# Reordering the first pass of a two-layer encoder kernel: c as one row, casts and loads in another order, eight gate dots moved into attention 0

## The chip, the cores and the metric

The kernel runs on one core of a Trainium2 chip. The metric is device time in microseconds (us), the median of three executions. The engines of a core work side by side and meet through semaphores: TensorE (PE; its weight loads are PEld), VectorE (DVE), ScalarE (ACT), GpSimd (POOL) and SyncE (SP), whose queue issues nearly all DMA transfers of this kernel.

## The reference

A trunk of two layers works on x (1024 tokens of 1024 values) with a conditioning vector c (1024 values). For layer i:

```
mod = silu(c) @ ada_w[i] + ada_b[i]          # 3 x 1024 values
shift, scale, gate = split(mod, 3)
h = rmsnorm(x, norm_g[i]) * (1 + scale) + shift
y = branch_i(h)                               # 0: differential attention, 1: latent attention
x = x + gate * y
```

Branch 0 projects h to q, k, v and z (1024 values each), rotates q and k by a position-dependent angle, takes for each of 8 heads the difference of two softmaxes, norms the result of each head, multiplies by silu(z) and projects out. A last RMSNorm closes the trunk. All data are float32.

## The kernel before, in words

A float32 product is made of three matmuls of a high and a low part in the `fp32r` format: high x high, high x low, low x high. So every operand is first split: ACT casts the high part, and POOL or VectorE subtracts it to get the low part (for weights L229/L230 and L547/L548, for h L493 to L498).

**The order of work.** The program text is the request; a scheduler then fixes the order of the instructions on each engine when the kernel is built, and `tc.issue_after(x)` asks it to place an instruction behind instruction x. At run time each engine takes its instructions in that fixed order and stops at the first one whose inputs are not ready. The SP queue works the same way: a DMA waits there for a free buffer and holds up what stands behind it. Tiles with a `tag` and `bufs=n` share n buffers in turn.

**First pass (L549 to L645).** It makes h for the first 512 tokens and, chunk by chunk of 128 channels (loop variable k), multiplies it into V for those tokens (`vacc`, four PSUM banks) and into the first half of the first K strip (`kacc`).

- c is loaded as 128 copies of one row (L424), tanh and one VectorE step make silu(c) times 2 (L427, L428), and ACT copies it into PSUM (`cb`, L559).
- x comes as four tiles of 128 tokens x 1024 (`load_x`). The sum of squares of each is taken on ACT or VectorE (`sq_x`), one POOL instruction makes the four inverse roots (`inv_rms`, `rsqrt`, L171), ACT scales the first 256 channels of each tile (L567), VectorE the other 768 (L621).
- For each k two weight tiles `ada` (512 KB each, four buffers) come in, and two dot products with c on VectorE (`mod_dot`, L434, inside `mod_pair`) give the shift and the scale of that chunk's 128 channels.
- `h_chunk` transposes the four tiles' channels of chunk k on PE (L488, bank `trh`) and makes h from them on ACT, twice: `h0h`, the high part (L493), and `h`, full precision (L495); POOL subtracts (`h0l`, L498). The V weights of chunk k are cast and subtracted as `wvh`, `wvl`.
- PE then does eight matmuls with h0h (L638, L639), two for K (L640, L641), four with h0l (L643) and one more for K (L644). The matmuls lag one chunk behind the transposes (SKEW).
- After the last chunk's dots VectorE turns positions into angles (`angles`, L575 to L592) and ACT takes three sines; the tables go to HBM and come back spread over partitions.

**After it.** The Q weights (`wq0`) are split and the Q strip of the first half is multiplied (`strip_half`, L184 to L186, into `acc`), for which the first `vacc` bank must be empty: `store_v` casts it on ACT (L361), subtracts on VectorE (L362) and stores it. The second 512 tokens are two tiles `xt` and two tiles cut in halves `xth`; their squares are all taken on ACT, all four inverse roots made at once and all of them scaled on VectorE (`norm_x`, L477). Then follow chunk by chunk their h and V.

**V stage.** The other half of V (weights `wv1`, outputs `vps`) is made tile by tile (`v0_tile`), beside K and Q strips of head 0. `gen_mods` runs along: one `mod_dot` of VectorE and one 512 KB load at each step, first 16 for layer 1's shift and scale, then 8 for layer 0's gate (`gen_gate`); MODS says how many steps go ahead of each V tile.

**Attention 0 (`attn0`, `q_tile`).** For each tile of 128 queries of a head PE makes two score tiles (L773, banks `sc`, two of them), VectorE takes the maximum of each (L399), ACT the exponential (L401), and VectorE combines the two (reciprocal L779, L780, combine L781). The result is transposed on PE (L382), moved out on ACT (`pth`, L384) and VectorE (`ptl`, L385), and multiplied with V (`pv`) for two tiles together. Between these, PE gets matmuls of the next head's strips as filling. `extra`, if given, is called after each tile. `mk["V"]` holds the last marked VectorE instruction, and `behind("V")` asks for a place behind it. Later stages (output projections, layer 1, attention 1) are not touched.

Of the kernel before, what the change touches and what calls it, by code (L numbers as in the profile page):

```python
# [21 lines left out]
P = 128  # L22
# [23 lines left out]
MODS = (2, 2, 2, 2, 3, 2, 0, 0)  # L46
# [14 lines left out]
VB = (2, 3)  # L61
WV1 = 6
ADA_B = 4
X1_AT = 6
WQ_AT = 6
# [3 lines left out]
X_CUT = 256  # L69
FIN_LAG = 1  # L70
# [15 lines left out]
def trunk(ctx: ExitStack, tc: tile.TileContext, A, out):  # L86
# [96 lines left out]
    def mm3(psum, ah, al, bh, bl, first, last):  # L183
        PE.matmul(psum, ah, bh, start=first, stop=False)  # L184
        PE.matmul(psum, ah, bl, start=False, stop=False)  # L185
        PE.matmul(psum, al, bh, start=False, stop=last)  # L186
# [17 lines left out]
    def fetch_strip(srcs, nks):  # L204
        raws = []
        for src, nk in zip(srcs, nks):
            raw = wst.tile([P, HF], F32, name="wraw", tag="wraw", bufs=2)
            SP.dma_start(raw[:, : nk * P], src)
            raws.append((raw, nk))
        return raws  # L210
# [148 lines left out]
    def store_v(l, sp, acc, tt, fh, tag="vst", bufs=None):  # L359
        v = sp.tile([P, 2, HF], F32R, name="v_hl", tag=tag, bufs=bufs or VB[l])  # L360
        S.copy(v[:, 0, :], acc)  # L361
# [54 lines left out]
    def mod_load(src, mp, nb, tag="ada"):  # L416
        w = mp.tile([P, D], F32, name="ada", tag=tag, bufs=nb)
        SP.dma_start(w, src)
        return w

    def load_c(pl, th, **kw):

        c2 = pl.tile([P, D], F32, name="c2", **kw)
        SP.dma_start(c2, A["c"].to_broadcast([P, D]))  # L424

        def fin():
            S.activation(th, c2, AF.Tanh, scale=0.5)  # L427
            V.scalar_tensor_tensor(out=c2, in0=th, scalar=1.0, in1=c2, op0=ALU.add, op1=ALU.mult)  # L428

        return c2, fin  # L430
# [13 lines left out]
    def gen_gate(l, load, c2):  # L444

        gcol = sm.tile([P, KT], F32, name="gcol", tag="gcol", bufs=1)
        for j in range(KT):
            mod_dot(load(A[f"ada_g{l}"][j]), part(f"ada_bg{l}")[:, j : j + 1], gcol[:, j : j + 1], c2)
            if j == KT - 1:
                SP.dma_start(gateS[l].rearrange("(p j) -> p j", p=P), gcol)  # L450
            yield

    def gen_mods(load, c2):
# [8 lines left out]
        yield from gen_gate(0, load, c2)  # L462
# [16 lines left out]
    def h_chunk(l, xn4, k, dst, hp, sub=G, wide=False, act=False, f32=None):  # L479
# [13 lines left out]
        S.activation(hh, tr[:, :n, :], AF.Identity, bias=bk, scale=ak)  # L493
        if act:
            S.activation(tmp, tr[:, :n, :], AF.Identity, bias=bk, scale=ak)  # L495
# [15 lines left out]
    st1 = ExitStack()  # L511
    p1 = pool(st1, "p1a")

    def load_x(half):

        xs = []
        for j in range(4):
            if half == 1 and j > 1:
                xs.append([wp.tile([P, HF], F32, name="xth", tag="rp", bufs=6) for _ in range(2)])
            else:  # L520
                xs.append([p1.tile([P, D], F32, name="xt", tag="xt", bufs=6)])
            for i, x_ in enumerate(xs[j]):
                n = D // len(xs[j])
                SP.dma_start(x_, A["x"][half * 4 + j, :, i * n : i * n + n])
        return xs

    def sq_x(xs, on_act=range(4)):
        ss = sm.tile([P, 4], F32, name="xss")
        for j, x_ in enumerate(xs):
            for i, piece in enumerate(x_):  # L530
                dst = ss[:, j : j + 1] if i == 0 else sm.tile([P, 1], F32, name="xs2")
                if j in on_act:
                    junk = p1.tile([P, D], BF16, name="junk", tag="junk", bufs=1)
                    S.activation(junk[:, : piece.shape[1]], piece, AF.Square, accum_out=dst)
                else:
                    junk = p1.tile([P, D], BF16, name="junk2", tag="h32", bufs=2)
                    V.tensor_tensor_reduce(out=junk, in0=piece, in1=piece, scale=1.0, scalar=0.0, op0=ALU.mult, op1=ALU.add, accum_out=dst)
                if i:
                    V.tensor_add(ss[:, j : j + 1], ss[:, j : j + 1], dst)
        return ss  # L540

    def load_wv(l, k, fh, src, eng=G):
        raw = p1b.tile([P, HF], F32, name="wvr", tag="wvr", bufs=2)
        SP.dma_start(raw, src)
        h_ = p1b.tile([P, HF], F32R, name="wvh", tag="wv", bufs=16)
# [5 lines left out]
    psum("ps1", accx=3, tr=1, cb=1)  # L551
    th = p1.tile([P, D], F32, name="cth", tag="ada", bufs=ADA_B)
    c2, c_fin = load_c(p1b, th)
    xs0 = load_x(0)
    posi = p1.tile([P, 256], I32, name="posi", tag="rot", bufs=3)
    SP.dma_start(posi, A["pos"])
    c_fin()
    cb = bank("cb", "cb", [P, D])
    S.copy(cb, c2)  # L559

    def ada0(j):
        return [mod_load(A["ada_ss0"][j, i], p1, ADA_B) for i in range(2)]

    wm0 = ada0(0)
    y0 = inv_rms(sq_x(xs0, X_ACT0), 4)
    for j in range(4):
        S.mul(xs0[j][0][:, :X_CUT], xs0[j][0][:, :X_CUT], y0[:, j : j + 1])  # L567


    tabS = [dr.tile([4, 32, 256], F32, name=f"tabS{i}") for i in range(3)]  # L570

    def angles():
        ang = p1.tile([P, 256], F32, name="ang", tag="rot", bufs=3)
        kk = p1.tile([P, 256], F32, name="kk", tag="rot", bufs=3)
        V.tensor_copy(ang, posi)  # L575
        V.tensor_scalar(ang, ang, inv[:, 0:1], None, op0=ALU.mult)
        MAGIC = float(1.5 * 2 ** 23)
# [6 lines left out]
        for C in (C1, C2, C3):  # L584
            V.scalar_tensor_tensor(out=ang, in0=kk, scalar=-C, in1=ang, op0=ALU.mult, op1=ALU.add)
# [24 lines left out]
    for k in range(-1, KT + SKEW):  # L610
# [11 lines left out]
        if k == KT - 1:  # L622
            with tc.issue_after(m_last):
                angles()
# [1218 lines left out]
```

## Time and profile before

| | us |
|---|---|
| median of three runs | 1441.18 |
| lowest and highest | 1438.9, 1443.01 |
| the profiled execution | 1438.65 |
| its span | 1436.9 |

The span runs from the first to the last instruction of the profiled execution. A row of a timeline holds start, length, engine, line, operation, output<-input, shapes and, in brackets, how long the engine had stood idle and what ended that. A row of the waits holds who waited for whom, the total in us, how often, and the longest.

### The profile page before, as it was taken

What the parts mean: (1) busy time and instruction counts of PE and PEld (TensorE: products, weight loads), DVE (VectorE), ACT (ScalarE), POOL (GpSimd) and SP (SyncE); (2) the same over time, 40 slices, a digit from 0 to 9 for tenths busy, and PEclk for the clock granted to TensorE, in tenths of its full rate; (3) what the DMA queues carried; (4) which work ended last, traced back from release to release, by engine and by line L of the source; (5) the groups of instructions that cost most, each with busy time, mean ns of one, the idle gap of its engine ahead of it and who ended that gap; (6) DMA issues with size and microseconds to landing.
All of it is one profiled execution on the core that took longest, in us unless ns stands there. A gap on an engine that the chain in (4) does not pass through costs nothing. (4 is left out here: it accounts for less than half of the span.)

```text
span 1436.9 us, 20644 instructions
## 1 busy us (share of the span) xinstructions
PE 1388.8 (97%) x7388; PEld 1158.8 (81%) x7388; DVE 917.5 (64%) x1372; ACT 728.7 (51%) x1287; POOL 610.6 (42%) x483
## 2 busy tenths in 40 slices
PE   5999999999999999998999999999999999999997
PEld 4778788888888888887787877887888888888886
DVE  6656877767777767677435985545666555555355
ACT  5622375666565656566343452335455554545342
POOL 4416164656464646464461343532141331412572
PEclk9999999999999999999999999999999999999999
DMA  8787723333332333237653145398343432336563
GB/s 326 238 254 237 255 70 93 84 104 81 96 101 84 96 89 91 86 96 248 236 183 125 38 132 184 122 305 236 133 130 111 130 101 77 104 96 217 185 237 136
DMA packets 135527, 213.70 MB, mean 149 GB/s; under 512 B 19072, under 2 KB 56064, under 8 KB 135424
## 3 DMA queue, kind: packets, MB, share of 16 engines
q1 hardware_dynamic: 135424, 212.38, 47.1%
q8 instruction: 58, 0.95, 0.3%
q14 instruction: 45, 0.37, 0.1%
HBM read 137.92 MB, written 50.80 MB: 131 GB/s over the span
## 5 line engine op out<-in xcount | busy, mean ns | idle before, releaser
L384 ACT CAST pth<-tr 128x512 fp32r<-128x512 f32 x256 | 150.6, 588 | 284.2 <-PE tr L382 281.9
L399 DVE TENSOR_REDUCE nm<-s 128x1 f32<-128x1024 f32 x192 | 234.1, 1219 | 77.2 <-PE s L773 65.7
L385 DVE TENSOR_TENSOR ptl<-tr,pth 128x512 fp32r<-128x512 f32 x256 | 176.2, 688 | 139.4 <-ACT pth L384 138.9
L230 POOL TENSOR_TENSOR wl<-wraw,wh 128x512 fp32r<-128x512 f32 (+2 forms) x79 | 103.6, 1314 | 205.6 <-ACT wh L229 183.4
L401 ACT ACTIVATE e<-s,nm 128x1024 f32<-128x1024 f32 x128 | 143.7, 1123 | 29.8 <-DVE nm L399 29.2
L382 PE MATMUL tr<-ident,e 128*128 128x128 f32 x1024 | 155.1, 274 | 2.3 <-DVE ptl L385 2.0
L382 PEld LDWEIGHTS tr<-ident,e 128*128 128x128 f32 x1024 | 121.2, 140 | 43.6 <-DVE ptl L385 19.2
L184 PE MATMUL acc<-h0h,wh 128*128 128x512 f32 x360 | 150.1, 417 | 1.9 <-DVE v_hl L362 1.8
L184 PE MATMUL pv<-pth,vt 128*128 128x256 f32 x512 | 147.1, 287 | 0.0
L185 PE MATMUL pv<-ptl,vt 128*128 128x256 f32 x512 | 145.8, 285 | 0.0
L186 PE MATMUL pv<-pth,vt 128*128 128x256 f32 x512 | 144.7, 283 | 0.0
L186 PE MATMUL acc<-h0h,wl 128*128 128x512 f32 x360 | 143.1, 398 | 0.5 <-POOL wl L230 0.5
L185 PE MATMUL acc<-h0l,wh 128*128 128x512 f32 x360 | 142.0, 394 | 0.0
L1013 POOL TENSOR_TENSOR wol<-wor,woh 128x512 fp32r<-128x512 f32 x64 | 85.0, 1351 | 84.7 <-ACT woh L1012 77.2
L185 PEld LDWEIGHTS pv<-ptl,vt 128*128 128x128 f32 x512 | 97.6, 191 | 2.9
L184 PEld LDWEIGHTS pv<-pth,vt 128*128 128x128 f32 x512 | 97.4, 190 | 2.9 <-ACT pth L384 0.2
L186 PEld LDWEIGHTS pv<-pth,vt 128*128 128x128 f32 x512 | 97.6, 191 | 0.1
L326 POOL TENSOR_TENSOR rp_r<-rp_raw,cosT 128x512 f32<-128x512 f32 x38 | 49.8, 1311 | 91.0 <-ACT rp_raw L321 50.8
L331 POOL TENSOR_TENSOR rp_sw<-rp_sw,sinT 128x512 f32<-128x512 f32 x42 | 55.4, 1318 | 74.1 <-DMA rp_sw<-rp_raw 73.9
L773 PE MATMUL s<-ks,qa 128*128 128x512 f32 x256 | 82.6, 404 | 2.8 <-DVE e L781 2.6
L781 DVE SCALAR_TENSOR_TENSOR e<-s,z,e 128x1024 f32<-128x1024 f32 x64 | 82.1, 1283 | 2.1
L773 PE MATMUL s<-ks,qb 128*128 128x512 f32 x256 | 81.1, 395 | 0.0
(590 smaller groups left out, 3335.4 us busy)
## 6 DMA issues: line engine op xcount, KB each, us to landing
ada<-in_ada_ss SPq DMA_DIRECT2D x32, 512.0 KB, 6.0
wraw<-in_w_s SPq DMA_DIRECT2D x64, 256.0 KB, 2.9
vS<-v_hl SPq DMA_DIRECT2D x32, 512.0 KB, 5.9
vt<-vS SPq DMA_DIRECT2D x32, 512.0 KB, 3.7
wor<-in_w_out SPq DMA_DIRECT2D x64, 256.0 KB, 3.9
rp_sw<-rp_raw SPq DMA_DIRECT2D x168, 64.0 KB, 2.0
bc_s<-bc_d SPq DMA_DIRECT2D x34, 256.0 KB, 4.1
oS<-bc_s SPq DMA_DIRECT2D x30, 256.0 KB, 2.5
```

The costliest lines, as they stand in the source:

```text
L184: PE.matmul(psum, ah, bh, start=first, stop=False)
L185: PE.matmul(psum, ah, bl, start=False, stop=False)
L186: PE.matmul(psum, al, bh, start=False, stop=last)
L230: sub = (V if pair_of else G).tensor_sub(l_[:, :n], raw[:, :n], f32v(h_[:, :n]))
L382: PE.transpose(tr[:, j, :], p[:, kt * P : (kt + 1) * P], ident)
L384: mk["S"] = S.copy(pth[kh][:, :, dst], tr).ins
L385: mk["V"] = V.tensor_sub(ptl[kh][:, :, dst], tr, f32v(pth[kh][:, :, dst])).ins
L399: mk["V"] = V.reduce_max(nm, s_ps, axis=AX.X, negate=True).ins
L401: mk["S"] = S.activation(e, s_ps, AF.Exp, bias=nm, scale=1.0, accum_out=zs).ins
L773: PE.matmul(s_ps[:, kc * HF : (kc + 1) * HF], src[:, c, ql], KS[h][kc][:, c, :], start=fst, stop=not fst)
L781: combined.append(V.scalar_tensor_tensor(out=e0, in0=e1, scalar=z1[:, 0:1], in1=e0, op0=ALU.mult, op1=ALU.add).ins)
L1013: in_turn(G.tensor_sub(lo, raw, f32v(hi)))
```

## The change

- **c.** It is loaded as one row of 4 KB (`crow`), silu is made on that row, and two matmuls with a row of ones spread it over 128 partitions into `cb`. A copy `c2` back to SBUF is made later, on ACT in chunk 5. Eight matmuls of ones are put ahead of the spread and nine behind it (`keep_busy`, WARM); their results are not used.
- **x, first half.** Squares and inverse roots are made for three tiles together, and for the fourth alone, with its square in two halves, one on ACT and one on VectorE. Of VectorE's four scalings two are placed behind the first pair of dots and two behind the second.
- **Angles and sines.** The positions are loaded in chunk 0; the VectorE steps are dealt out over five chunks, the sines over chunks 4, 5 and 7 (SIN_AT).
- **Order of loads and casts.** Many loads and casts get an `issue_after`: V and K weights are split behind the h of the chunk before, the Q weights are loaded ahead of the second half's x, and the V weights wv1 from the fourth on are split behind the copies of the V banks.
- **x, second half.** The squares of the first two tiles go to VectorE, those of the other two stay on ACT; inverse roots and scalings are made for each pair by itself, and the second half of the channels of the second pair is scaled on ACT.
- **Gate dots.** The eight dots of layer 0's gate leave the V stage and are called from attention 0, one after every fifth tile, through `extra`. c2 and two load buffers get a pool of their own (`pg`) that stays open until attention 0 is over.
- VB gives V's stores three buffers instead of two, and the scratch for dynamic DMAs is set to 1024.

```
-MODS = (2, 2, 2, 2, 3, 2, 0, 0)
+MODS = (2, 1, 1, 1, 0, 0, 0, 0)
-VB = (2, 3)
-WV1 = 6
+VB = (3, 3)
+WV1 = 3
+WARM = (8, 9)
+SIN_AT = (4, 5, 7)
...
+    def sq_halves(pieces, dst):
+        other = sm.tile([P, 1], F32, name="xs2")
+        sq_piece(pieces[0], dst, True)
+        sq_piece(pieces[1], other, False)
+        V.tensor_add(dst, dst, other)
...
-    c2, c_fin = load_c(p1b, th)
-    xs0 = load_x(0)
+    warm = bank("acc", "warm")
+    SP.dma_start(crow[0:1, :], A["c"])
+    xs0 = [load_x(0, 0)]
+    xs0 += [load_x(0, j) for j in range(1, 4)]
+    keep_busy(WARM[0])
...
+    c_act = S.activation(th[0:1, :], crow[0:1, :], AF.Tanh, scale=0.5).ins
+    c_last = V.scalar_tensor_tensor(out=crow[0:1, :], in0=th[0:1, :], scalar=1.0, in1=crow[0:1, :], op0=ALU.add, op1=ALU.mult).ins
+    cb = bank("cb", "cb", [P, D])
+    for f in range(2):
+        fs = slice(f * HF, f * HF + HF)
+        spread = PE.matmul(cb[:, fs], ones[0:1, :], crow[0:1, fs], start=True, stop=True).ins
+    with tc.issue_after(spread):
+        keep_busy(WARM[1])
...
+    y_ = inv_rms(ss0[:, 0:3], 3)
+    for j in range(3):
+        y0[j] = y_[:, j : j + 1]
+        S.mul(xs0[j][0][:, :X_CUT], xs0[j][0][:, :X_CUT], y0[j])
+    sq_halves([xs0[3][0][:, :HF], xs0[3][0][:, HF:]], ss0[:, 3:4])
+    y0[3] = inv_rms(ss0[:, 3:4], 1)[:, 0:1]
...
             with tc.issue_after(m_last):
-                for j in range(4):
-                    V.tensor_scalar(xs0[j][0][:, X_CUT:], xs0[j][0][:, X_CUT:], y0[:, j : j + 1], None, op0=ALU.mult)
-        if k == KT - 1:
+                x_rest(0)
+                x_rest(1)
+        if k == 0:
             with tc.issue_after(m_last):
-                angles()
+                x_rest(2)
+                x_rest(3)
...
+            if k >= 0:
+                with tc.issue_after(m_last):
+                    next(angle_steps, None)
...
+            if k + 1 < KT:
+                with tc.issue_after(h_chunk.act):
+                    wv0.append(split_wv(vraw))
+            if k in SIN_AT:
+                sines(SIN_AT.index(k))
...
-    norm_x(sq_x(xs1), xs1)
+    norm_x(ssa, xs1[:2])
+    yb = inv_rms(ssb, 2)
+    for j in range(2):
+        V.tensor_scalar(xs1[2 + j][0], xs1[2 + j][0], yb[:, j : j + 1], None, op0=ALU.mult)
+        S.mul(xs1[2 + j][1], xs1[2 + j][1], yb[:, j : j + 1])
...
+    def gate_steps0():
+        gcol = sm.tile([P, KT], F32, name="gcol", tag="gcol", bufs=1)
+        yield
+        w = []
+        for j in range(KT):
+            while len(w) < min(2, KT - j):
+                with tc.issue_after(mod_load.last):
+                    w.append(mod_load(A["ada_g0"][j + len(w)], pg, 2))
+            for _ in range(5):
+                yield
+            js = slice(j, j + 1)
+            with behind("V"):
+                mod_dot(w.pop(0), part("ada_bg0")[:, js], gcol[:, js], c2)
+        SP.dma_start(gateS[0].rearrange("(p j) -> p j", p=P), gcol)
+
+    gate0 = gate_steps0()
     for h in range(NH - 1):
-        attn0(h, lambda i: FILL0[i])
+        attn0(h, lambda i: FILL0[i], lambda i: next(gate0, None))
```

201 lines of the change are left out of this document (117 added, 84 removed).

## The prediction

> **What bounds the kernel now.** I read the page's busy shares first, then busy time by stage, then what TensorE waited for, then the timeline around each wait. Columns of the stage table: stretch, length, busy time of PE, PEld, DVE, ACT, POOL, granted clock, DMA share, GB/s.
>
> ```profile
> PE 1388.8 (97%) x7388; PEld 1158.8 (81%) x7388; DVE 917.5 (64%) x1372; ACT 728.7 (51%) x1287; POOL 610.6 (42%) x483
> ...
> 14.46:23.30 8.84, 7.75 (x24) 5.04 (x24) 8.77 (x13) 5.19 (x10) 5.96 (x4) 1.00 0.86 324
> 49.17:55.06 5.89, 3.69 (x10) 2.38 (x10) 2.56 (x6) 4.73 (x13) 1.26 (x1) 0.71 0.61 184
> 300.00:350.00 50.00, 50.00 (x280) 42.55 (x279) 33.53 (x50) 30.72 (x54) 30.76 (x26) 1.00 0.31 89
> ...
> PE trh L488 <- ACT xt L567: 14.5, 1, 14.5
> PE vacc L643 <- POOL h0l L498: 2.1, 1, 2.1
> ...
> PE vps L184 <- ACT wvh L547: 0.7, 1, 0.7
> ...
> PE vps L185 <- DVE wvl L548: 0.2, 1, 0.2
> ```
>
> PE is busy 97% of the span, so only its idle time and its slow matmuls can be won. The change touches the front: 14.5 us before the first transpose, a stretch to 23.3 us with VectorE full (8.77 of 8.84) and PE half empty, and a hole at 49 us. In attention 0 PE has no idle time, while VectorE is busy for two thirds: whatever is moved there has to fit into VectorE's gaps.
>
> **The change part by part. The start.**
>
> ```profile
> 3.00:6.00 3.00, 0.00 (x0) 0.00 (x0) 0.00 (x0) 0.00 (x0) 0.00 (x0) 1.00 0.97 231
> 6.00:9.00 3.00, 0.00 (x0) 0.00 (x0) 1.45 (x2) 2.58 (x4) 0.00 (x0) 1.00 1.01 410
> 11.23 1.23 DVE L537 CUSTOM_DVE_ANT_0 junk<-xt 128x1024 bf16<-128x1024 f32 x1 [1.22 <-DMA xt<-in_x]
> 12.82 1.04 POOL L171 TENSOR_TENSOR rq_y<-xss,mhalf 128x4 f32<-128x4 f32 x1 [11.54 <-DVE xss L466]
> 13.90 1.71 ACT L567 ACTIVATE xt<-xt,rq_y 128x256 f32<-128x256 f32 x4 [2.67 <-POOL rq_y L171]
> 15.52 0.62 DVE L621 TENSOR_SCALAR xt<-xt,rq_y 128x768 f32<-128x768 f32 x1
> 16.20 1.59 POOL L548 TENSOR_TENSOR wvl<-wvr,wvh 128x512 fp32r<-128x512 f32 x1 [2.34 <-ACT wvh L547]
> 18.14 1.64 DVE L621 TENSOR_SCALAR xt<-xt,rq_y 128x768 f32<-128x768 f32 x1
> 22.28 1.27 DVE L434 CUSTOM_DVE_ANT_0 ada<-ada,cb,vec 128x1024 f32<-128x1024 f32 x1
> 22.46 0.78 ACT L493 ACTIVATE h0h<-trh,modb,moda 128x512 fp32r<-128x512 f32 x1 [3.29 <-DVE moda L442]
> 23.30 0.50 PE L638 MATMUL vacc<-wvh,h0h 128*128 128x512 f32 x1 [0.18 <-ACT h0h L493]
> 27.28 0.39 PE L638 MATMUL vacc<-wvh,h0h 128*128 128x512 f32 x1
> 43.89 1.39 DVE L575 CAST ang<-posi 128x256 f32<-128x256 int32 x1
> 52.44 0.64 ACT L534 ACTIVATE junk<-xth 128x512 bf16<-128x512 f32 x1
> 52.98 0.19 ACT L534 ACTIVATION_READ_ACCUMULATOR junk<-xth 128x1 f32 x1
> ```
>
> The spread copy of c (512 KB) goes; 4 KB take its place. At 410 GB/s its bytes are 1.3 us; but the engines were full at 231 GB/s from 3 to 6 us, another 1.3 us lost to slow packets. I take 2.3 us (bounds 1.3 and 2.6): the last token tile, awaited until 11.23, lands at 8.9. Its square is now cut in halves of 512 columns (0.64 and 0.19 on ACT, the other half beside it on VectorE); the inverse root for three tiles and then that for the fourth each take POOL 1.04, so the fourth tile is scaled at 12.5 (four scalings took 1.71, one 0.43) against 15.6. The first pair of dots (2 x 1.27 and small steps) starts when its first weights land, 512 KB or 1.3 us behind x at 10.2, and ends at 13.25.
>
> From there VectorE's order decides. Two scalings of the rest of x (0.62, and 1.64 next to a POOL instruction, as in the rows): 15.5. The second pair, 2.75: 18.3, against 22.4 before (ACT got the result at 22.46). But then come, ahead of the third pair, the cast of the positions (1.39), two more scalings (0.62 and 1.64) and one small step (0.35): 4.0, so 22.3; third pair 25.1; the h of the third chunk 0.8 later. The transposes of the third chunk stand in PE's order behind three matmuls of the second and need all four scalings, so PE, which reaches them at about 20.2, idles for 2.1 us. The third chunk's matmuls start at 26.0 against 27.28: gain **1.3 us**, not the 3 that the second chunk would have had. Bounds: with c worth only 1.3 us, 0.3; with no contention between POOL and VectorE, some 3. The 17 warm matmuls, the two that spread c, the rows of c on ACT and VectorE and the copy of c out of PSUM lie in time in which those engines have nothing else, and cost nothing; the SP queue has one DMA as before. The wait of the vS store, and of loads ordered behind others, holds nothing that PE needs within its 2 us lead.
>
> **The end of the first half.** From the third to the eighth chunk PE has no gap before (27.28 to 46.74, five chunks, 3.89 each) and I leave that: the eighth starts at 45.5.
>
> ```profile
> 46.74 0.39 PE L638 MATMUL vacc<-wvh,h0h 128*128 128x512 f32 x1
> 48.78 0.39 PE L641 MATMUL kacc<-h0h,wl 128*128 128x512 f32 x1
> 49.12 0.76 ACT L495 ACTIVATE h<-trh,modb,moda 128x512 f32<-128x512 f32 x1
> 51.28 1.93 PE L643 MATMUL vacc<-wvh,h0l 128*128 128x512 f32 x4 [2.10 <-POOL h0l L498]
> 51.96 0.59 ACT L361 CAST v_hl<-vacc 128x512 fp32r<-128x512 f32 x1 [1.16 <-PE vacc L643]
> 52.00:53.00 1.00, 1.00 (x3) 0.71 (x3) 0.42 (x1) 1.00 (x3) 0.00 (x0) 0.50 0.75 178
> 52.58 0.69 DVE L362 TENSOR_TENSOR v_hl<-vacc,v_hl 128x512 fp32r<-128x512 f32 x1 [2.89 <-ACT v_hl L361]
> 53.73 0.79 PE L184 MATMUL acc<-h0h,wq 128*128 128x512 f32 x1
> 59.96 0.38 PE L488 MATMUL trh<-ident,xt 128*128 128x128 f32 x2
> 61.43 0.50 PE L184 MATMUL vacc<-wvh,h0h 128*128 128x512 f32 x1 [0.43 <-ACT h0h L493]
> ```
>
> Before, ACT made the last h at 49.12, behind squares and sines, POOL followed, PE stood 2.1 us and then ran at a granted clock of 0.50. The change puts sines and casts of the weights into earlier chunks and the squares behind the h. What is late next is the emptying of the first V bank (ACT 0.59, DVE 0.69), which the Q matmuls wait for. From the start of the eighth chunk: ten matmuls of 0.23, the first of the last four 0.39, then 0.59 and 0.69 with 0.1 between: 4.2 us to the first Q matmul, against 6.99 (46.74 to 53.73): gain **2.75**. The 24 Q matmuls at full clock take 24 x 0.233 = 5.6 us against 6.23: **0.6**.
>
> **The pairs of the second half.**
>
> ```profile
> 56.40 1.01 POOL L171 TENSOR_TENSOR rq_y<-xss,mhalf 128x4 f32<-128x4 f32 x1 [5.17 <-DVE xss L466]
> 58.78 1.67 DVE L477 TENSOR_SCALAR xth<-xth,rq_y 128x512 f32<-128x512 f32 x4
> ```
>
> The second pair's four squares (0.64 and 0.19 each, as above) stand on ACT between the bank copies (0.58), so they can't start before the V banks are done: 8.3 us after the eighth chunk's start; sums, POOL's 1.01 and two scalings of 0.42 bring it to 10.8, while PE is through with Q at 9.8. Then two more scalings and a bank copy stand on ACT before the first h (12.55). From the last Q matmul to the first V matmul: 2.75 us against 1.47 (59.96 to 61.43): **-1.3**. The first pass together: 1.3 + 2.75 + 0.6 - 1.3 = 3.35 us.
>
> **The V stage.** Eight dots (10.9 us of VectorE) and 4 MB leave it. Two of its waits hang on V weights that were fetched late (0.7 and 0.2, the two vps rows above); the Q half now stands ahead of them on PE. A third (1.13) is for the emptying of a bank, which stood on VectorE behind gate dots and a reduction:
>
> ```profile
> 159.65 0.50 PE L184 MATMUL acc<-h0h,wh 128*128 128x512 f32 x1 [1.13 <-DVE v_hl L362]
> ```
>
> Gain **2.0** if all three go (bounds: 0, where other waits follow in their place, and these 2.0).
>
> **The dots in attention 0.** Eight of 1.36 us (with the read), one in every fifth tile, placed between the second evacuation of a tile and the reciprocal that waits for ACT's exponential.
>
> ```profile
> 190.46 0.16 DVE L779 RECIPROCAL z<-z 128x1 f32<-128x1 f32 x1 [0.41 <-ACT s L401]
> 310.09 1.28 DVE L781 SCALAR_TENSOR_TENSOR e<-s,z,e 128x1024 f32<-128x1024 f32 x1
> 311.99 0.63 PE L773 MATMUL s<-ks,qa 128*128 128x512 f32 x2
> ```
>
> In the usual tile VectorE waits 0.41 us there, so the combine (L781) is moved by 1.0. Half of the dots fall on a tile after which PE has its P x V matmuls (24) and needs that bank only 4 us later: free. Behind the other four the next scores follow the combine's end by about 0.6 (310.09 + 1.28 to 311.99): 0.4 to 0.5 us each, unless the tile already had spare time. I take **-1.0** (bounds: 0, and 8 x 1.36 = -10.9). The loads (8 of 512 KB at a DMA share of 0.31) are hidden; each waits on SP for a buffer that the dot of two turns earlier freed.
>
> **Sum.** 3.35 + 2.0 - 1.0 = 4.35 us. The profiled execution took 1438.65 (span 1436.9); 1434.3. It lies 2.5 below the median of the runs, 1441.18; so 1436.8 for the median.
>
> **The clock, by page and by row.** The hole of 2.1 us at 49 us was followed by 0.50; a hole as long at 891 us was not:
>
> ```profile
> 893.01 0.50 PE L186 MATMUL zacc<-t2h,wl 128*128 128x512 f32 x1 [2.12 <-POOL wl L230]
> ```
>
> [...]
>
> **Rivals.**
> 1. *The clock drops in the new holes.* A drop lasts about 3.6 us at half speed, as from 51.3 to 55.0: 1.85 us lost. One or both of them take the first pass to 1.5 or -0.4; with V and dots the gain is 0.6 to 2.5: 1439.6. For it: the 2.1 us hole is as long as the one that had it. Against: the hole at 891.
> 2. *The dots stall attention 0.* Place: VectorE between evacuation and reciprocal; price: up to 1.36 each, since the next reduction, the exponential and the evacuation of the one transpose bank all queue behind it. Slower than before from 0.67 us a dot on (5.35 / 8); at the full price 10.9 - 5.35 = 5.5 slower: 1446.7. For it: PE has no slack of its own there. Against: half of the places have 4 us.
> 3. *The start is better than worked out.* If POOL and VectorE do not collide behind the second pair and the token chain keeps its 2.3 us, the third chunk starts at 24.2, 1.8 earlier, and the pairs' squares run ahead (1.3 back): 1433.7.
> 4. *The change does nothing where it aims:* the last h still comes late, behind the casts of the Q weights that stand ahead of it on ACT (1.13), if those land late: the 2.75 goes, 1439.6.
>
> **Chances.** Forecast 0.50 (its own range 1434 to 1439), rival 1 0.15, rival 2 0.11, rival 3 0.16, rival 4 0.08. 0.3% (4.3 us) is about what a measurement of this kernel can tell from no change. Faster by more: half of the forecast, rival 3 and a little of the others: 0.45; slower by more: rival 2, and a little: 0.12; within: 0.43. The range goes from 1430.5 (rival 3 with all V waits gone and no stall) to 1443 (rival 1 with 0.6 us a dot), leaving 0.2 out.
>
> **What the profile after would show.** The first chunk's h near 13.5 us; a PE wait for x's scalings near 20 to 22; the third chunk from 26; no POOL wait before the last four V matmuls, the first Q matmul near 50 with clock 1.00; a wait of 1 us for xth at 56; no wait for V weights near 90; short waits of the scores for the combine in attention 0, at every other dot. Wrong would make me: a clock under 1.00 at 22 or 58, a late landing of the last modulation weights, or more than 3 us of PE idle in attention 0.

## The result, and the profile after

The changed kernel took 1437.68 us (median of 14 runs, 1434.67 to 1441.94) against 1441.66 for the kernel before (14 runs, 1438.72 to 1445.61): 4.0 us less, a ratio of 0.9970 (95% interval 0.9958 to 0.9982). The forecast was 1436.8, 4.4 less than before. Its profiled execution took 1437.65 (span 1435.9), right at its median, while the profiled execution of before (1438.65) was shorter than any of those 14; the two profiles differ by 1.0 us only, and the medians tell the truer difference.

The page's busy shares of the changed kernel:

```profile
PE 1398.5 (97%) x7426; PEld 1165.9 (81%) x7426; DVE 921.5 (64%) x1377; ACT 727.2 (51%) x1287; POOL 612.9 (43%) x485
```

Its busy time by stage, the same stretches and columns as in the prediction:

```profile
14.46:23.30 8.84, 7.92 (x36) 5.85 (x37) 8.77 (x16) 3.68 (x8) 6.66 (x6) 1.00 1.03 393
49.17:55.06 5.89, 5.89 (x29) 4.79 (x28) 3.50 (x10) 4.60 (x11) 0.70 (x1) 1.00 0.79 206
300.00:350.00 50.00, 50.00 (x283) 42.71 (x283) 36.71 (x56) 30.42 (x54) 30.86 (x26) 1.00 0.31 85
```

Between 14.46 and 23.30 TensorE now issues 36 matmuls where it issued 24; at 49 us the hole and the half clock are gone (5.89 of 5.89 busy, clock 1.00); from 300 to 350 us, in attention 0, VectorE has 3 us more work and TensorE still no idle time.

The timeline of the start of the changed kernel, then that of the end of the first half (start, length, engine, line and operation; in brackets the idle time before and what ended it):

```profile
9.10 0.69 DVE L513 CUSTOM_DVE_ANT_0 junk<-xt 128x512 bf16<-128x512 f32 x1 [1.28 <-DMA xt<-in_x]
13.69 0.78 ACT L473 ACTIVATE h0h<-trh,modb,moda 128x512 fp32r<-128x512 f32 x1 [0.59 <-DVE xt L605]
18.93 0.28 DVE L561 CAST ang<-posi 128x256 f32<-128x256 int32 x1
19.13 0.61 DVE L605 TENSOR_SCALAR xt<-xt,rq_y 128x768 f32<-128x768 f32 x1
19.66 0.34 DVE L562 TENSOR_SCALAR ang<-ang,vec 128x256 f32<-128x256 f32 x1
19.92 0.61 DVE L605 TENSOR_SCALAR xt<-xt,rq_y 128x768 f32<-128x768 f32 x1
24.11 0.50 PE L693 MATMUL vacc<-wvh,h0h 128*128 128x512 f32 x1
44.77 0.39 PE L693 MATMUL vacc<-wvh,h0h 128*128 128x512 f32 x1
47.46 0.59 ACT L362 CAST v_hl<-vacc 128x512 fp32r<-128x512 f32 x1 [3.41 <-PE vacc L698]
47.94 0.63 ACT L511 ACTIVATE junk<-xth 128x512 bf16<-128x512 f32 x1
48.83 0.50 PE L185 MATMUL acc<-h0h,wq 128*128 128x512 f32 x1 [0.50 <-DVE v_hl L363]
51.75 0.21 ACT L511 ACTIVATION_READ_ACCUMULATOR junk<-xth 128x1 f32 x1
53.17 1.34 ACT L714 ACTIVATE xth<-xth,rq_y 128x512 f32<-128x512 f32 x2 [1.21 <-POOL rq_y L172]
54.53 0.38 PE L468 MATMUL trh<-ident,xt 128*128 128x128 f32 x2
56.00 0.50 PE L185 MATMUL vacc<-wvh,h0h 128*128 128x512 f32 x1 [0.43 <-ACT h0h L473]
```

The last x tile is there at 9.10 (11.23 before), the first h at 13.69, the third chunk at 24.11 (27.28), the eighth at 44.77 (46.74), the first Q matmul at 48.83 (53.73), the first V matmul of the second half at 56.00 (61.43). Up to here 5.4 us are won. What TensorE waited for in the V stage of the changed kernel (56 to 166 us: total, times, longest):

```profile
PE s L847 <- ACT e L402: 1.6, 1, 1.6
PE acc L185 <- DVE v_hl L363: 1.6, 2, 1.0
PE vps L185 <- DVE gz L782: 1.4, 1, 1.4
PE acc L187 <- POOL wl L231: 0.6, 1, 0.6
```

From its timeline, the last of these waits:

```profile
160.87 1.11 ACT L402 ACTIVATE e<-s,nm 128x1024 f32<-128x1024 f32 x1 [1.74 <-DMA vS<-v_hl]
162.12 0.74 PE L847 MATMUL s<-ks,qa 128*128 128x512 f32 x2 [1.61 <-ACT e L402]
```

The waits for late V weights are gone, as is the one for the bank behind the gate dots at 159 us. In their place stand a wait of 1.35 for a PSUM bank (gz) and one of 1.61 for an exponential that itself waited for a store of V, and the waits for a bank that v_hl empties have grown (0.54 and 1.02, where the kernel before has 0.65 at this place): 5.1 us in all, against 3.3 in the kernel before.

### The profile page after: what moved, and what is told of

Same layout as the page of the kernel before. It is cut to its first block, busy times and chain, and to the rows that moved or that the text cites. A ratio compares the mean times of both kernels' runs of the same rounds, so it can differ in the third digit from the quotient of the medians.

```text
span 1435.9 us, 20702 instructions
## 1 busy us (share of the span) xinstructions
PE 1398.5 (97%) x7426; PEld 1165.9 (81%) x7426; DVE 921.5 (64%) x1377; ACT 727.2 (51%) x1287; POOL 612.9 (43%) x485
## 5 line engine op out<-in xcount | busy, mean ns | idle before, releaser
L231 POOL TENSOR_TENSOR wl<-wraw,wh 128x512 fp32r<-128x512 f32 (+2 forms) x79 | 105.1, 1333 | 205.1 <-ACT wh L230 170.1
L187 PEld LDWEIGHTS acc<-h0h,wl 128*128 128x128 f32 x360 | 67.6, 188 | 16.3 <-POOL wl L231 1.0
```

What stands on the lines that cost most here:

```text
L187: mm3.last = PE.matmul(psum, al, bh, start=False, stop=last).ins
L231: sub = (V if pair_of else G).tensor_sub(l_[:, :n], raw[:, :n], f32v(h_[:, :n]))
```

## The experiments

All times of a variant are medians, set against runs of the kernel before made beside them on the same chip. The table follows landmarks through the profiles of all variants: by how many us each stands earlier than in the first profile of before (there: third chunk 27.28, first Q matmul 53.73, first V matmul of the second half 61.43, 35th P x V matmul 196.66, 545th 556.88, 749th 689.29; all are starts of TensorE rows of the timeline). The difference from the third to the fourth column of numbers is what the V stage gave or took, from the fourth to the fifth attention 0 as far as its dots reach, from the fifth to the sixth the end of attention 0. The column behind them is the time of the profiled execution itself: each row of landmarks is one execution, and those of sines_late and gate_only were the longest of all runs of their kernel (4.7 and 5.3 us above the median).

| variant | 3rd chunk | Q | 2nd half | PxV 35 | PxV 545 | PxV 749 | profiled | median less before | ratio (95%) |
|---|---|---|---|---|---|---|---|---|---|
| before, again | 0.12 | 0.27 | 0.40 | -0.50 | -0.43 | -0.84 | 1440.86 | | |
| changed | 3.17 | 4.90 | 5.43 | 4.76 | 4.64 | 2.25 | 1437.65 | -4.0 | 0.9970 (0.9958-0.9982) |
| changed, again | 2.73 | 5.09 | 5.64 | 5.32 | 5.20 | 3.98 | 1434.09 | -4.2 | 0.9969 (0.9955-0.9982) |
| c_spread | -2.46 | -0.23 | 0.31 | -0.46 | -0.62 | -1.15 | 1439.8 | +0.3 | 1.0004 (0.9990-1.0017) |
| no_warm | 1.54 | 4.19 | 4.74 | 4.89 | 4.84 | 4.29 | 1434.48 | -6.1 | 0.9958 (0.9942-0.9974) |
| sines_late | 3.25 | 1.82 | 0.83 | -0.26 | -0.37 | -3.43 | 1444.84 | +0.4 | 1.0009 (0.9998-1.0020) |
| norm_four | 2.82 | 4.72 | 3.85 | 2.62 | 2.47 | 1.47 | 1437.22 | -4.3 | 0.9968 (0.9955-0.9981) |
| gates_back | 3.24 | 3.88 | 4.43 | -5.19 | -5.12 | -7.83 | 1445.68 | +6.1 | 1.0050 (1.0033-1.0068) |
| gate_only | 0.13 | 0.17 | 0.16 | -2.00 | -2.14 | -2.80 | 1442.76 | -3.3 | 0.9983 (0.9970-0.9996) |
| dots_twice | 3.06 | 5.00 | 5.52 | 1.94 | 0.79 | -2.14 | 1443.8 | +1.2 | 1.0002 (0.9987-1.0016) |
| no_dots | 2.67 | 4.17 | 4.71 | 4.13 | 4.16 | 0.47 | 1436.51 | -3.7 | 0.9975 (0.9963-0.9988) |
| e_turn | 2.66 | 4.44 | 4.97 | 6.11 | 5.97 | 2.54 | 1436.43 | -3.7 | 0.9972 (0.9961-0.9983) |
| e_turn_z_first | 2.60 | 4.04 | 4.58 | 6.20 | 6.06 | 5.29 | 1434.13 | -5.6 | 0.9965 (0.9952-0.9978) |

From the 749th P x V matmul to the end, a part that the change does not touch, these profiles take 745.9 to 750.6 us (747.6 in the first profile of before). So the end of one profile says little about a variant, and the medians have to say it.

**The two kernels again.**

> The changed kernel unaltered, executed and profiled a second time: 1437.7 within its own spread (1434.7 to 1441.9). What it is for: the two profiled executions of before and after are single samples. If the V stage's waits are fixed by the program, the waits of TensorE from 56 to 166 us add up to 5.1 us again (within 0.5) and those from 560 to 666 us to the same; if they hang on when transfers land, they differ by 1 us or more.

> The kernel before unaltered, profiled a second time: 1441 within its spread (1437 to 1446). If its first profile was a lucky one (it is 2.5 to 3 us under the median), the V stage (61 to 166 us) now has 2 us or more of waits above the 3.3 us seen there; if not, 3.3 again and the rest of the kernel is longer.

The changed kernel took 1436.46 (1432.3 to 1438.17), the one before 1440.86. The first pass repeats to within 0.4 us. In the V stage the wait for gz (1.35 again) and that for the exponential (1.51) come back, and the smaller ones come to 1.6 against 2.1: the total is 4.5. The kernel before has 4.7 us of V-stage waits this time, 1.4 more than in its first profile (a wait for V weights of 1.33 in place of 0.65, one for a bank of 1.28 in place of 0.65). So part of the waits is written into the program and another part, 0.6 us in sum for one kernel and 1.4 for the other, goes with the execution; a V stage of one profile is no better than that, and that of before was on the low side, if not by the 2 us that this expectation asked for.

**The row of c.**

```diff
-    SP.dma_start(crow[0:1, :], A["c"])
+    SP.dma_start(crow, A["c"].to_broadcast([P, D]))
-c_act = S.activation(th[0:1, :], crow[0:1, :], AF.Tanh, scale=0.5).ins
+c_act = S.activation(th, crow, AF.Tanh, scale=0.5).ins
```

(and the product behind it on 128 rows in the same way)

> The changed kernel with one part undone: c is loaded as 128 copies of its row (512 KB) again, in the same place at the head of the queue; all else as changed. By the prediction the last x tile lands 2.3 us later (bounds 1.3 and 2.6), and so do the first h and the third chunk: 1437.7 + 2.3 = 1440.0. Rival: the first pairs of dots and their weights set the third chunk and hide it: under 1 us.

1441.07, 0.3 above before: without the row of c the whole gain of the change is lost, 4.3 us, more than twice the 1.8 us by which the larger load delays x. The timeline of this variant shows where it goes:

```profile
10.91 0.69 DVE L513 CUSTOM_DVE_ANT_0 junk<-xt 128x512 bf16<-128x512 f32 x1 [1.22 <-DMA xt<-in_x]
20.59 1.42 POOL L534 TENSOR_TENSOR wvl<-wvr,wvh 128x512 fp32r<-128x512 f32 x1
20.78 1.65 DVE L605 TENSOR_SCALAR xt<-xt,rq_y 128x768 f32<-128x768 f32 x1
22.28 1.29 POOL L478 TENSOR_TENSOR h0l<-h,h0h 128x512 fp32r<-128x512 f32 x1 [0.26 <-ACT h L475]
22.35 1.37 DVE L562 TENSOR_SCALAR ang<-ang,vec 128x256 f32<-128x256 f32 x1
23.54 1.31 POOL L534 TENSOR_TENSOR wvl<-wvr,wvh 128x512 fp32r<-128x512 f32 x1
23.65 1.61 DVE L605 TENSOR_SCALAR xt<-xt,rq_y 128x768 f32<-128x768 f32 x1
25.32 0.33 PE L468 MATMUL trh<-ident,xt 128*128 128x128 f32 x1 [1.95 <-DVE xt L605]
```

And its stage view behind that wait:

```profile
26.50:29.50 3.00, 3.00 (x9) 2.32 (x8) 2.96 (x8) 1.55 (x3) 0.02 (x1) 0.50 0.64 183
```

The last x tile comes 1.8 us later than in the changed kernel (10.91 against 9.10). That shifts VectorE's three small instructions (L605, L562, L605) onto GpSimd's: 1.65, 1.37 and 1.61 where the changed kernel has 0.61, 0.34 and 0.61. TensorE waits 1.95 for the last of them, and after that wait the granted clock is 0.50. This is the hole of 2.1 us that the prediction put at 20 us, with the clock drop of its first rival: it is there, but only when c comes late. The third chunk comes 5.6 us after that of the changed kernel, and 5.1 are left at the first Q matmul.

**The warm matmuls.**

```diff
-WARM = (8, 9)
+WARM = (0, 0)
```

> The changed kernel without its 17 warm matmuls at the start (the two that spread c stay); all else as changed. By the prediction they cost nothing, and nothing was counted for them: 1437.2, within 0.7. Rival: they keep TensorE at full speed for the first chunk, whose first matmuls took 0.63 to 0.80 us each in the kernel before and 0.39 to 0.50 in the changed one; without them the first chunk ends some 2 us later, the third chunk starts 1 us or more later than 24.1, and so does the end. If the dots of the second chunk set the third one anyway, the slow matmuls show in the first chunk and the first Q matmul still stands near 48.8.

1434.48, 6.1 under before. The intervals of this ratio and of the changed kernel's overlap, so a gain from leaving them out is not shown; a loss of 2 us or more does not fit them. In its timeline the matmuls of the first chunk do take up to twice as long:

```profile
14.67 0.80 PE L693 MATMUL vacc<-wvh,h0h 128*128 128x512 f32 x1 [0.92 <-ACT h0h L473]
19.48 0.63 PE L695 MATMUL kacc<-h0h,wh 128*128 128x512 f32 x1
```

The third chunk starts at 25.74 (24.11), the Q matmuls at 49.54 (48.83), and 0.7 us remain at the second half; by the 35th P x V matmul nothing remains. In the second profile of the changed kernel the first chunk is as slow with the warm matmuls: their second group was done at 9.38, TensorE then stood 2.09 us before the first transposes, and from 14 to 18 us the granted clock is 0.50, with matmuls of 0.63 to 0.80; it lost nothing either (Q at 48.64).

**The sines.**

```diff
+        if k == KT - 1:
+            for n in range(3):
+                sines(n)
         if 0 <= k < KT:
             h_chunk(0, xs0, k, h0[k][0], p1, act=True)
...
-            if k in SIN_AT:
-                sines(SIN_AT.index(k))
```

> The changed kernel with one part undone: the sines, the copy of c out of PSUM and their table load go back ahead of the last h of the first half on ScalarE (before, the sines stood there). By the prediction this brings back the wait of POOL's h0l before the last four V matmuls (2.1 us) and the half clock behind it (0.6): the first Q matmul 2.75 us later than the changed kernel's 48.8, 1440 to 1441. Rival by the first profiles: a wait of that length need not halve the clock (one at 891 us did not): then the Q matmuls take 5.6 as in the changed kernel, and 2.1 to 2.75 are lost. If a later wait takes the loss in, as with the pairs undone (first V matmul of the second half 1.6 later, total unchanged), the total is within 1 us of the changed kernel.

1440.17, 0.4 above before: some 4 us are lost against the changed kernel, and no later wait takes them in. But the wait stands elsewhere than expected. The last h on ScalarE is late (44.28 against 41.57) and so is GpSimd's h0l, yet the last four V matmuls start only 0.5 later. It is VectorE behind them that breaks, in the timeline of this variant:

```profile
47.52 1.23 DVE L513 CUSTOM_DVE_ANT_0 junk<-xt 128x1024 bf16<-128x1024 f32 x1 [1.18 <-POOL h0l L478]
49.76 1.42 DVE L457 TENSOR_SCALAR xt<-xt,rq_y 128x1024 f32<-128x1024 f32 x2 [0.81 <-POOL rq_y L172]
51.16 1.88 DVE L363 TENSOR_TENSOR v_hl<-vacc,v_hl 128x512 fp32r<-128x512 f32 x3
51.91 0.80 PE L185 MATMUL acc<-h0h,wq 128*128 128x512 f32 x1 [2.96 <-DVE v_hl L363]
```

Its stage view behind the wait:

```profile
52.00:55.00 3.00, 3.00 (x7) 2.41 (x8) 2.15 (x7) 0.87 (x2) 0.70 (x1) 0.50 1.12 242
```

A square waits for the buffer that h0l is being made from, the scalings wait for its root, and the emptying of the V banks stands behind both: Q begins 3.1 us later (2.75 forecast) and at half clock, 4.6 at the second half. Both are of one execution, the longest of its runs; the median loses 4.4.

**The pairs.**

```diff
-    ssa, ssb = [sm.tile([P, 2], F32, name="xss") for _ in range(2)]
+    ssx = sm.tile([P, 4], F32, name="xss")
...            (all squares on ScalarE behind the last h)
-    norm_x(ssa, xs1[:2])
-    yb = inv_rms(ssb, 2)
...
+    norm_x(ssx, xs1)
```

> The changed kernel with the pairs undone: the squares of all four tiles of the second half on ScalarE behind the last h, one inverse root for the four, all scalings on VectorE, as before. By the prediction, which had the pairs at a loss of 1.3 against the order before, undoing them wins 1 us or changes nothing (1436.5 to 1437.7). By the trace after, in which two squares, a root and two scalings are done before the Q matmuls end, undoing them puts the first V matmul of the second half some 4 us later (ScalarE: 5.8 of squares and 2.9 of copies, then root 1.0 and scalings 3.2): 1441.

1436.32, 4.3 under before: the same as the changed kernel, as the prediction's side had it, but not for its reason. The pairs do win: without them the first V matmul of the second half is at 57.58, 1.6 later, since one root for four follows the last square and all scalings follow that on VectorE. In the V stage this grows to 2 to 3 us (a wait of 1.87 at 91 us has the granted clock at 0.50 for 3.4 us behind it), and at the 749th P x V matmul 0.8 to 2.5 are left; the medians show none of it. Where it is lost behind this point was not followed.

**The place of the first gate's dots.** Put back into the V stage of the changed kernel, and, the other way round, moved alone in the kernel before:

```diff
-MODS = (2, 1, 1, 1, 0, 0, 0, 0)
+MODS = (2, 2, 2, 2, 3, 2, 0, 0)
...
+        yield from gen_gate(0, load, c2)
...
-        attn0(h, lambda i: FILL0[i], lambda i: next(gate0, None))
+        attn0(h, lambda i: FILL0[i])
```

> The changed kernel with one part undone: the eight dots of the first gate go back into the V stage, none in attention 0. If the prediction's terms hold (V stage worth 2.0, dots in attention 0 cost 1.0), this is 1.0 us slower than the changed kernel and its P x V matmuls of attention 0 start 2 us later. If the dots' place is worth nothing (rival, from the trace after: no PE wait between 200 and 500 us where the dots stand, and other waits of 5.1 us in the V stage in place of 3.3), it is within 1 us. If the dots are what lost 2.6 us between 560 and 666 us of the changed kernel, it is 1.5 to 3 us faster and that stretch has 2.6 us less of PE waits.

> The kernel before with this one part alone: the first gate's dots leave the V stage for attention 0 (one in every fifth tile), all else as before. By the prediction's terms 1.0 us faster than before (2.0 less 1.0) and the wait of 1.13 at 159 us gone. If the dots' place is worth nothing: within 0.7 us of before, with other waits in the V stage. If dots in attention 0 stall PE: slower than before, with waits of the scores for the combine between 200 and 500 us.

gates_back took 1446.88: 10 us more than the changed kernel, and 6.1 more than before. gate_only took 1437.48: 3.3 less than before (2.4 by the ratio of the pairs). None of the expectations was near the first of these. In the profile of gate_only the waits of 1.13 and 0.21 at 160 and 165 us are gone, as expected; but TensorE waits 1.96 at 115 us for a copy on ScalarE, with the granted clock at 0.50 for 3.4 us behind it, and so this one execution stands 2.0 later at the 35th P x V matmul, while the median is faster. The timeline of gates_back at the end of the V stage:

```profile
157.70 1.28 DVE L865 SCALAR_TENSOR_TENSOR e<-s,z,e 128x1024 f32<-128x1024 f32 x1
159.12 0.70 PE L857 MATMUL s<-ks,qa 128*128 128x512 f32 x2 [3.97 <-DVE e L865]
162.39 1.28 DVE L424 CUSTOM_DVE_ANT_0 ada<-ada,c,vec 128x1024 f32<-128x1024 f32 x1 [1.05 <-DMA ada<-in_ada_g]
164.34 0.79 PE L185 MATMUL acc<-h0h,wh 128*128 128x512 f32 x1 [2.91 <-DVE v_hl L363]
```

Its stage view around these waits:

```profile
150.00:160.00 10.00, 6.03 (x27) 4.66 (x26) 9.82 (x14) 2.41 (x4) 0.00 (x0) 0.99 0.98 318
160.00:172.00 12.00, 9.09 (x28) 6.92 (x27) 8.49 (x14) 3.96 (x7) 0.00 (x0) 0.58 0.86 263
```

The gate's weights come last, in a stretch whose DMA share is 0.98 and 0.86. The first pass has brought TensorE to the V stage 4.4 us earlier; the weights have not come earlier (the last two dots start at 162.4 and 164.2 us here, at 160.0 and 161.5 in the kernel before). So the first scores of attention 0 now fall among the dots: from 150 to 160 us VectorE is busy for 9.82 of 10 us (8.07 in the kernel before), with five dots, four of them ahead of the first combine, and TensorE waits 3.97 us for that combine. The wait of 2.91 is for the emptying of a bank behind the dot at 162.39, which itself waits 1.05 for its weights. From 160 to 172 us the mean granted clock is 0.58. The V stage takes 9.6 us back. The two halves of the change do not add: the first pass without the move loses 6.1, the move without the first pass wins 2.4 to 3.3, both win 4.0.

**The dots in attention 0.**

```diff
-                mod_dot(w.pop(0), part("ada_bg0")[:, js], gcol[:, js], c2)
+                V.tensor_copy(gcol[:, js], w.pop(0)[:, 0:1])
```

(no_dots; dots_twice lets a second dot over the product follow each)

> The changed kernel without the eight dot products of the first gate in attention 0: each is replaced by a copy of one column (the gate's values are left out), and their loads stay. By the prediction the eight dots cost 1.0 us there, so this takes 1436.7. By the trace after, which has no wait where they stand, they cost nothing (1437.7, within 0.5) and the waits from 560 to 666 us stay. If they cost as much as doubling them did (4.3), 1433 to 1434.

> The changed kernel with each of the eight dots in attention 0 followed by a second one of the same size on VectorE (its result unused): twice the cost under dispute. By the prediction's 1.0 for eight dots, 1.0 or more slower (and up to 10.9 if VectorE has no slack there). By the trace after, which shows no PE wait where the dots stand: under 0.7 us, and the shift of P x V matmuls against the kernel before stays 4.6 us from 200 to 550 us.

Without dots 1437.0, within the spread of the changed kernel's 1437.68 and 1436.46. Where the dots stand (35th to 545th P x V matmul), the changed kernel loses 0.12 us in both profiles, no_dots nothing, dots_twice 1.15. The view of what TensorE waited for from 200 to 550 us has no row for the changed kernel; for dots_twice it has this one:

```profile
PE s L847 <- DVE e L855: 1.4, 2, 0.8
```

Eight dots fit into VectorE's gaps, sixteen do not quite. The 4 us that dots_twice loses in the median are more than these 1.4, and where the rest goes is not shown. Its profile (1.9 above its median) loses 3.6 us in the V stage and 2.9 behind the 545th matmul, where it has nothing that the changed kernel does not have; in both places the granted clock falls to 0.50 for 3.4 us (from 164.9 and from 666.6 us), as in neither profile of the changed kernel.

**The end of attention 0** (545th to 749th P x V matmul) takes 2.4 and 1.2 us in the two profiles of the changed kernel and 0.4 in the second of before, but 3.7 in no_dots, 0.6 in no_warm, 2.7 in gates_back and 0.5 in c_spread. It goes neither with the dots nor with the size of the lead. What the largest losses have in common is the clock: in no_dots, e_turn, sines_late, dots_twice and gates_back (2.7 to 3.7 us) the granted clock is 0.50 for 3.4 us somewhere between 661 and 676 us, in the other nine profiles (0 to 2.4 us) not once. By that clock 3.4 us do the work of 1.7, an estimate. The stage view of no_dots:

```profile
664.50:667.50 3.00, 3.00 (x16) 3.00 (x15) 1.37 (x2) 2.40 (x6) 0.00 (x0) 0.50 0.85 322
```

The rest is short waits. One of them, in the timeline of the changed kernel and, behind it, of the first profile of before:

```profile
628.53 1.29 POOL L332 TENSOR_TENSOR rp_sw<-rp_sw,sinT 128x512 f32<-128x512 f32 x1 [6.29 <-DMA rp_sw<-rp_raw]
629.79 1.53 POOL L885 TENSOR_TENSOR o<-o,bc_s 128x512 f32<-128x512 f32 x1
629.85 2.01 DVE L336 TENSOR_TENSOR rp_r<-rp_r,rp_sw 128x512 f32<-128x512 f32 x1
633.62 0.73 PE L847 MATMUL s<-ks,qa 128*128 128x512 f32 x2 [1.32 <-DVE e L855]
```

```profile
630.17 1.30 POOL L331 TENSOR_TENSOR rp_sw<-rp_sw,sinT 128x512 f32<-128x512 f32 x1 [4.11 <-DMA rp_sw<-rp_raw]
633.49 0.68 DVE L335 TENSOR_TENSOR rp_r<-rp_r,rp_sw 128x512 f32<-128x512 f32 x1
```

A rotation's transfer lands 2 us later in its tile, VectorE's sum then falls on a GpSimd instruction (2.01 in place of 0.68), and the scores wait 1.32 for the combine behind it. A wait for the combine at this tile stands in the second profile of the changed kernel too (0.74), in neither of the kernel before. Why the transfer is later was not tried.

**The two waits that took the place of the old ones.** The pool that holds the modulation weights has three buffers in rotation, and the last two V tiles are stored from it. With 13 loads ahead of them (before) they fall into the second and third buffer; with five (the change) into the third and first. The pool of attention 0 lies over the same memory, and its first exponential goes over the first buffer: over the V tile that is stored last. e_turn takes two turns more of the rotation; e_turn_z_first also puts Z of head 0 ahead of the first rotations.

```diff
         if tt == V_LATE:
+            for _ in range(2):
+                V.memset(pm.tile([P, D], F32, name="ada", tag="ada", bufs=3)[:, 0:4], 0.0)
...            (e_turn_z_first alone:)
-    for t in pend[:4]:
-        t()
     turn = 0
     stream0.step(Z_PRE)
+    for t in pend[:4]:
+        t()
```

> The changed kernel with two unused turns in the rotation of the three buffers that hold the modulation weights and then the last two V tiles (two four-element fills on VectorE), so that the first exponential of attention 0 is not put over the V tile that is stored last. If the wait of TensorE for that exponential (1.6 us at 160 us, behind the landing of that store) comes from this overlap, which the eight dots fewer brought about by moving the rotation on, it goes, and the P x V matmuls stand 1.5 us earlier: 1435.7. If the exponential is late for another reason (VectorE, the landing of V), the wait stays: 1437.2.

> As e_turn, and the gate of head 0 (Z) is put ahead of the first rotations of K and Q in the program: its product on VectorE then stands ahead of the rotation's sum that waits for GpSimd. The wait of 1.35 us at 122 us, for a PSUM bank that this product empties, should go too: 1.5 + 1.35 = 2.85 us under the changed kernel, 1434.3. Rival: the bank is late because of ScalarE's table load, and 0.3 or less is won; or K and Q of head 0 come later and the first scores wait.

What TensorE waited for from 56 to 166 us (the rows of 1 us or more), first in e_turn, then in e_turn_z_first:

```profile
PE vps L185 <- DVE gz L782: 1.4, 1, 1.4
PE acc L185 <- DVE v_hl L363: 1.3, 2, 1.1
```

```profile
PE acc L185 <- DVE v_hl L363: 2.5, 3, 1.7
```

The wait for the exponential is gone in both, the one for gz in the second; there a bank that is emptied behind the first exponentials costs 1.67 at 153 us (it was no wait in e_turn). The V stage gives 1.1 and 1.6 us where it took 0.3 to 0.7 in the changed kernel. The medians are 1436.08 (-3.7) and 1434.13 (-5.6; five runs). The profiles thus show the cause of both waits; that the second variant is faster than the changed kernel is likely (1434.13 against 1437.68 and 1436.46), but the intervals of the ratios overlap. It and no_warm are the fastest kernels run; the two edits together were not run.

## Why the prediction was right

The time came out within 0.9 us of the forecast and the difference within 0.4, with the sign as given; at 0.28% it lies just inside the 0.3% that the chances were set against. But of the six terms of its sum two were right, and the errors of the others cancel: that the number is so close is luck. The mechanism that came is the one of rival 3 for the whole first pass, start and pairs, for which the prediction had 1433.7; it is the V stage that brings the time back to the forecast.

- **Start, +1.3 forecast; 3.2 and 2.7 in two profiles.** The arrival of x was right (8.9 forecast, 9.10), as was the first h (13.5, 13.69). The step that failed is the 4.0 us of casts and scalings next to GpSimd, with TensorE idle for 2.1: they took 1.6 (18.93 to 20.53) without any collision. c_spread shows that the collision is real (1.65, 1.37 and 1.61 us for instructions that take 0.61, 0.34 and 0.61 in the changed kernel), and that arriving 1.8 us earlier is what avoids it. This was the start of rival 3 (24.2 for the third chunk). The forecast had the instructions right and the phase of the two engines wrong; it also took c at 2.3 where, with the collision that it saves, it is worth 4.3 in the median. The sum also counts no clock drop behind the holes that it expects; that was the author's estimate, and the runs show both: a granted clock of 0.50 behind a wait of 1.95 us in c_spread, of 1.00 behind one of 2.10 in the second profile of before.
- **Chunks three to eight, unchanged at 3.89.** They took 4.13 each (24.11 to 44.77), so that the lead at the eighth was 2.0 in place of 3.2. The sines with their table load (1.28 us, at 33.01) stand in this part now; that they cause it was not tried.
- **End of the first half, +2.75 and +0.6: right.** 4.06 us from the eighth chunk to the first Q matmul (4.2 forecast, 6.99 before), and the first to the last Q matmul in 5.46 (5.99 before). sines_late gives back 3.1 at Q and some 4 in the median; rival 4 (casts of the Q weights) did not come, and up to there, the first chunk of the second profile aside, the clock stayed at 1.00.
- **Pairs, -1.3 forecast; 0, and 1.4 better than without them.** The prediction had the squares through 8.3 us after the eighth chunk's start, the second pair scaled at 10.8 and Q done at 9.8. In the profile squares and copies alternate, as it said, but the step that failed is their length: a copy and a square take 1.1 us together from start to start (47.46, 48.57, 49.66, 50.75) and not the 1.4 that their rows add up to (8.3 is 2.7 to the first copy and four times 1.4), because the rows of one engine overlap: the copy at 47.46 lasts 0.59, the square behind it begins at 47.94. The last square is through at 51.96, 7.2 after the eighth chunk's start; the two halves are then scaled side by side on ScalarE and VectorE, done at 54.51, just as Q is (54.53). From there to the second half's first V matmul it is 1.47 us in both kernels, 2.87 in norm_four.
- **V stage, +2.0; -0.7 and -0.3.** The three waits went, as said, but others came in their place. The prediction had named that case with a gain of 0 as its lower bound, and did not take it; the measured values lie below even that. One, the exponential over the last V tile, is an effect of the edit that no profile of before could show: eight loads fewer move a rotation of three buffers.
- **Dots in attention 0, -1.0; -0.1.** VectorE's gaps hold all eight. The step that failed is half a us for every second place: the tiles had the spare time that the prediction mentioned as the exception, and the short waits of the scores for the combine, which it expected at every other dot, are not there.

At the 545th P x V matmul this adds up to 4.6 and 5.2 us, against 4.35 forecast: 2.1 and 2.3 more from the first pass, 2.7 and 2.3 less from the V stage, 0.9 more from the dots. The end of attention 0 then takes 1.2 to 2.4 back, an item that the sum did not have, and which differs from execution to execution; in the first pair of profiles another 1.25 goes behind it.

What the sum could not say is what gates_back shows: the terms were treated as independent, while this first pass is only worth something because the gate's dots and their weights no longer have to come in the V stage.

## What to carry to other kernels

A lead of 4.4 us into the V stage came out of it as 5.2 us of loss where the gate's weights were still due there (gates_back): see which loads are last in the next saturated stage before you count a lead, and undo one half of a change at a time. When a change alters how many tiles a rotating pool hands out, see which buffers the tiles behind it and the next pool fall on (here a wait of 1.61 us, gone in e_turn). What VectorE lost next to GpSimd went by phase: with x 1.8 us later (c_spread) a scaling took 1.61 to 1.65 in place of 0.61, and the median was 4.3 us longer, so a contention taken from a trace belongs in the bounds and not in the sum.

## What the runs showed of the hardware that was not expected

- *Waits of about 2 us, with and without a drop of TensorE's clock behind them.* The granted clock was 0.50 after waits of 1.95 (c_spread, 25 us), 2.10 (before, 49 us), 2.96 (sines_late, 49 us) and 2.09 (changed kernel's second profile, 9 to 11 us). It stayed at 1.00 after 2.10 at the same place in the second profile of before, and after 2.12 at 891 us in the first; there the second profile has 0.50 after 2.11. A drop lasted 3.4 us (before, 51.5 to 54.9), or longer: 6.8 (12.4 to 19.2 in the changed kernel's second profile) and 10.3 (159.8 to 170.1 in gates_back). The stage view of that second profile of before, to be set beside the row of 52 to 53 us (0.50) in the prediction:

```profile
52.00:55.00 3.00, 2.13 (x9) 1.13 (x8) 2.08 (x4) 3.00 (x9) 0.00 (x0) 1.00 0.87 242
```

So the same wait of the same program, 2.10 us, had the drop in one execution and not in the other. What decides between the two is not shown.
- *The clock column need not show a slow start.* In no_warm the stage view (below) gives a clock of 1.00 from 14 to 18 us, while its 512-column matmuls take 0.63 to 0.80 us (rows above) against 0.39 to 0.50 in the first profile of the changed kernel; in the second profile of the changed kernel, with the same lengths, the column says 0.50. Lengths of rows are the safer reading there:

```profile
14.00:18.00 4.00, 3.33 (x9) 2.42 (x10) 4.00 (x5) 2.31 (x4) 4.00 (x3) 1.00 1.04 420
```
- *VectorE and GpSimd side by side.* The same scaling of 128 x 768 takes 0.61 alone and 1.61 to 1.65 next to a GpSimd instruction, a sum of 128 x 512 takes 0.68 and 2.01. In the four such rows above VectorE's instruction ends 0.15 to 0.54 us behind the end of the GpSimd instruction into which it started (22.43 and 22.01 in c_spread, 631.86 and 631.32 in the changed kernel); whether it ran slower or waited the other out is not shown.
